# Eight experts of a mixture on one core: three at 128 slots and five at 64 in place of four and four

## The chip, the core and the metric

The kernel runs on one core of a Trainium2 chip. The metric is the device time of one execution in microseconds (us). Before the change the median of three runs is 1869.29 us (1868.2 to 1874.53). The core's engines are TensorE (PE; PEld loads its stationary operand), VectorE (DVE), ScalarE (ACT), GpSimd (POOL) and SyncE (SP), which here only issues loads. A load or store runs on the core's 16 DMA engines.

## The reference

Two layers of a diffusion transformer on 256 latent and 256 context tokens of width 1024, all in 32-bit floating point. The first layer has neighbourhood attention, a convolution and a dense feed-forward block; the second has a state-space mixer and, at its end, a mixture of eight experts on the 256 latent tokens. Only this last part is touched:

```
def moe_swiglu(h, w_router, w1, w3, w2):
    t = h.reshape(-1, shp[-1])                     # 256 x 1024
    logits = t @ w_router                          # 256 x 8
    top_val, top_idx = lax.top_k(logits, 2)
    top_w = jax.nn.softmax(top_val, axis=-1)
    gate = ...                                     # 256 x 8, zero but for two experts per token
    for e in range(8):
        out = out + gate[:, e:e+1] * swiglu(t, w1[e], w3[e], w2[e])

swiglu(h, w1, w3, w2) = (silu(h @ w1) * (h @ w3)) @ w2
```

The weights of an expert are two matrices of 1024 x 3584 and one of 3584 x 1024, 44 MB, so the eight have 352 MB. Each token goes to two experts. With the reference's inputs the experts get 116, 34, 59, 57, 98, 34, 91 and 23 tokens, in the order of the weights.

## The kernel before, in words

**Slots and places.** Each expert's tokens are gathered into a fixed number of slots, 128 or 64. Which place of the program has how many is the table `FEW` (true: 64 slots, here called narrow; false: 128, wide). Place 0 is always expert 0; the other places take the other experts by the number of their tokens. `arrange` ranks the counts on VectorE, `place_rank` holds the rank that each place takes, and `cap` its number of slots. The weights of the places 1 to 7 are loaded by an index that SyncE reads from `cnt` (`moe_src`). What goes beyond the slots of a place is computed in a second pass (`overflow`), which runs only if there is something. Before, `FEW` alternates: places 0, 2, 4 and 6 are wide.

**Steps.** An expert is worked in seven steps, its chunks of 512 hidden columns. A step reads six units of 1 MB: two of w1, two of w3 (the up products) and two of w2 (the down products). The two kinds of step differ:

- In a wide step each unit is split into a rounded high part (ScalarE, line 203) and the rest (mostly VectorE, line 205), and every product is three matmuls with 512 columns (`mm3`, lines 223 to 225): 72 in all. A unit's buffer is free once it is split.
- In a narrow step the units are used as they are, in full 32-bit matmuls. Two of them with 64 stationary columns lie side by side in the array: w1 beside w3 in the up products (line 2022), the two halves of the width in the down products (line 2056). A unit's buffer is free once its matmuls are done.

The list of all steps, `self.steps`, is made in `moe_plan`, and the order of the loads (`seq`) follows from it. In that order a step's w2 units stand after the next step's w1 and w3. Before, the list begins with `LAG` = 2 wide steps and then takes one wide and one narrow step in turn, while there are wide ones. It ends with two narrow steps more.

**Order of the work.** `moe` walks the list. For step i it issues the first up products, the transposes of the hidden values of step i-1 (`turn`), the second up products, and the down products of step i-1 (`finish`). The orders of TensorE, ScalarE, GpSimd and SyncE are those of the program; VectorE's is the scheduler's. `need` splits a wide step's units up to two units ahead. At given chunks of an expert it prepares the next one of its kind: its permutation is turned for the way back at chunk 2 (`way`), the next expert's permutation is built at chunk 4 (`place`, on GpSimd), and its tokens are fetched at chunk 6 (`gather`: lines 1850 wide, 1868 narrow). After an expert's last down products its results are weighted and added back to the residual in six parts (`scatter`, `scatter_few`, matmuls at 1915, 1916 and 1940, additions on VectorE at 1922), one part at each of three calls of `step()` per step.

**Loads.** `Stream` issues every unit from SyncE's queue into the next free buffer (line 85): four of its own and six lent by stages that are done, ten of 1 MB in all in this stage. The queue is strictly in order, and waits where the next buffer isn't free:

```
    def issue(self):
        while self.free and self.at < len(self.specs):
            which = self.free.pop(0)
            ...
                self.nc.sync.dma_start(view, src)
    def release(self, name):
        ...
        self.free.append(which)
        self.issue()
```

Of the kernel before, what the change touches and what calls it, by code (L numbers as in the profile page):

```python
# [9 lines left out]
F32 = mybir.dt.float32  # L10
# [3 lines left out]
OP = mybir.AluOpType  # L14
AX = mybir.AxisListType
P = 128
# [140 lines left out]
class Kernel:  # L157
# [1495 lines left out]
    def route_first(self):  # L1653

        nc, a = self.nc, self.a
        G = nc.gpsimd
        flat = self.pw.rearrange("p a b c -> p (a b c)")
        at = [128]

        def new(*shape):  # L1660
            n = int(np.prod(shape))
            v = flat[:, at[0]:at[0] + n]
            at[0] += n
            return v if len(shape) == 1 else v.rearrange("p (a b) -> p a b", a=shape[0])
        self.iota, self.before, self.ones = new(P), new(P), new(P)
        self.tri, self.router, self.lift = new(8, 8), new(8, 8), new(8, 8)
        self.gate, self.mask, self.pos, self.lg, self.rank = (new(2, 8) for _ in range(5))
        self.base, col, self.ssq, self.v01 = new(8), new(2, 8), new(2, 2), new(2, 2)
        pattern = lambda o, p, m: G.iota(o, pattern=p, base=0, channel_multiplier=m,
                                         allow_small_or_imprecise_dtypes=True)  # L1670
        pattern(self.iota, [[1, P]], 0)
        pattern(self.tri, [[1, 8], [-1, 8]], 0)
        pattern(self.before, [[1, P]], -1)
        G.tensor_scalar(self.tri, self.tri, 0.0, None, op0=OP.is_gt)
        G.tensor_scalar(self.before, self.before, 0.0, None, op0=OP.is_gt)
        G.memset(self.ones, 1.0)
        o = self.s5u.tile([P, 336], F32, name="order")
        self.iota64, self.hot = o[:, 0:P], o[:, P:P + 64].rearrange("p (a b) -> p a b", a=8)
        self.own = [o[:, 192 + 16 * i:208 + 16 * i].rearrange("p (a b) -> p a b", a=2) for i in range(3)]
        self.place_rank, self.cap, self.sums, self.ranks = (o[:, 240 + 8 * i:248 + 8 * i] for i in range(4))  # L1680
        pattern(self.iota64, [[0, 2], [1, 64]], 0)
        pattern(self.place_rank, [[1, 4], [4, 2]], 0)
        G.iota(self.cap, pattern=[[0, 4], [-64, 2]], base=P, channel_multiplier=0, allow_small_or_imprecise_dtypes=True)
        G.tensor_scalar(self.cap[:, 0:1], self.cap[:, 0:1], FIRST, None, op0=OP.add)
        G.dma_start(self.router, a["router"])
        for i in range(2):
            G.dma_start(col[:, i], self.rowsd[i + 1:i + 2].rearrange("a (k p) -> p (a k)", p=P))
        G.tensor_tensor(self.lift, self.router, col[:, 0][:, :, None].to_broadcast([P, 8, 8]), op=OP.mult)
        G.tensor_tensor(self.router, self.router, col[:, 1][:, :, None].to_broadcast([P, 8, 8]), op=OP.mult)
# [146 lines left out]
    def place(self, e, t, beyond=False):  # L1836

        pos, mask = (self.own[i][:, t, e:e + 1] if e or beyond else (self.pos, self.mask)[i][:, t, 0:1] for i in range(2))
        if beyond:
            p = self.wk([P, 1], "ss", 4)  # L1840
            self.nc.gpsimd.tensor_scalar(p, pos, -64.0 if FEW[e] else -float(P), None, op0=OP.add)
            pos = p
        eng = self.nc.gpsimd if e else self.nc.vector
        eng.tensor_scalar(self.perm[:, e % 2, t], self.iota64 if FEW[e] and not beyond else self.iota, pos, mask, op0=OP.is_equal,  # L1844
                          op1=OP.mult)

    def fetch(self, pt, n, t, e=0):

        for i in range(4):
            self.nc.tensor.matmul(pt[:, i * P:(i + 1) * P], lhsT=self.h2[:, t, (4 * n + i) * P:(4 * n + i + 1) * P],  # L1850
                                  rhs=self.perm[:, e % 2, t].bitcast(F32), start=not t and not i, stop=t == 1 and i == 3,
                                  skip_group_check=True)

    def fetched(self, pt, n):
# [18 lines left out]
    def way(self, e):  # L1873

        nc = self.nc
        back = self.back[:, e % 2]
        pt = self.ps("bk")
        for t in range(2):
            nc.tensor.transpose(pt[:, t * P:(t + 1) * P], self.perm[:, e % 2, t].bitcast(F32), self.ident)  # L1879
        nc.scalar.copy(back.rearrange("p a b -> p (a b)"), pt[:, 0:256])  # L1880
        return back

    def gather(self, e, beyond=False):
# [4 lines left out]
        def rest():  # L1888
            if FEW[e] and not beyond:
                self.fetch_few()  # L1890
                return
            for n in range(2):
                pt = self.ps("xT")
                for t in range(2):
                    self.fetch(pt, n, t, e)
                self.fetched(pt, n)
# [70 lines left out]
    def moe_plan(self):  # L1967

        many, few = ([(e, c) for e in range(8) if FEW[e] == i for c in range(7)] for i in range(2))
        self.steps = many[:LAG]  # L1970
        for i, s in enumerate(few):
            self.steps += many[LAG + i:LAG + i + 1] + [s]
        seq, last = [], []
        for e, c in self.steps:
            seq += [(k, e, c, j) for j in range(2) for k in ("m1", "m3")] if FEW[e] else \
                   [(k, e, c, j) for k in ("m1", "m3") for j in range(2)]
            seq += last
            last = [("m2", e, c, j) for j in range(2)]
        seq += last
        for s in seq:  # L1980
            self.st.add(s, partial(self.moe_src, *s))
        self.mseq = seq
        self.expert = {}
# [7 lines left out]
    def moe(self):  # L1991
        nc = self.nc
        seq = self.mseq
        pos = {s: i for i, s in enumerate(seq)}

        def need(name):
            i = pos[name]
            for j in (i, i + 1, i + 2):
                if j < len(seq) and not FEW[seq[j][1]]:
                    self.split(seq[j])  # L2000
# [67 lines left out]
        few = self.hT.rearrange("p k t -> p (k t)")[:, 0:1024].rearrange("p (a b) -> p a b", a=2)  # L2068
        self.few = few[:, 0].rearrange("p (k s) -> p k s", k=8)
        held, y, adds, after = None, {}, [], {}  # L2070
# [6 lines left out]
        def finish(e, c, t):  # L2077
            if not c:
                y[e] = self.ps("y") if FEW[e] else [self.ps("y") for _ in range(2)]
            down(e, c, t, y[e])  # L2080
            if c == 6:
                ready, add = (self.scatter_few if FEW[e] else self.scatter)(e, y.pop(e), self.back[:, e % 2])
                acts = [partial(ready, 0), partial(ready, 1) if FEW[e] else partial(ready, 1, "ntmp")] + \
                       [partial(add, n, (u,)) for n in range(2) for u in range(2)]
                adds.extend([acts[i] for i in v] for v in ADDS)
        end = len(self.steps) - 1
        for i, (e, c) in enumerate(self.steps):
            if FEW[e]:
                o = self.ps("m1")
                up_few(e, c, 0, o)  # L2090
                ready_h = lambda o=o: self.hidden_few(o)
            else:
                p1 = up("m1", e, c)
            step()
            if i:
                t = turn(*held)
            else:
                self.weights()
                self.arrange()
                for p in range(1, 8):  # L2100
                    self.expert[p] = nc.values_load(self.cnt[0:1, 16 + p:17 + p], engines=[mybir.EngineType.SP],
                                                    min_val=0, max_val=7)
            if i == 1:
                after[1] = self.gather(1)
            if c == 2:
                self.way(e)
            if c == 4 and e < 6:
                after[e % 2] = self.gather(e + 2)
            if FEW[e]:
                up_few(e, c, 1, o)  # L2110
            else:
                p3 = up("m3", e, c)
                ready_h = lambda p1=p1, p3=p3: self.hidden(p1, p3)
            step()
            early = not c or i == end
            if early:
                held = e, ready_h()
            if i == LAG:
                after[1]()
            if c == 6 and e < 6:  # L2120
                after[e % 2]()
            if i:
                finish(*self.steps[i - 1], t)
                step()
            if not early:
                held = e, ready_h()
        finish(7, 6, turn(*held))
        while adds:
            step()
# [157 lines left out]
START = ((1, 3), (1, 3), (1, 3), (3, 1))  # L2287
SPLIT1 = (2, 3)

FEW = (False, True) * 4  # L2290

LAG = 2

FIRST = 1024.0

# [27 lines left out]
```

## Time and profile before

| | us |
|---|---|
| median of three runs | 1869.29 |
| profiled execution, its own time | 1870.19 |
| its span, from the first to the last instruction | 1868.4 |
| TensorE busy (8730 matmul records) | 1725.3, 92% |
| VectorE busy | 1249.1, 67% |
| ScalarE busy | 803.0, 43% |
| loads and stores | 517.08 MB, mean 277 GB/s |
| loads of expert weights | 336 units of 1 MB |

Busy shares are means over the whole span. The expert stage is its second half: its first matmul starts at 986.13 us, its first narrow matmul at 1034.7 us. What a change in that stage is worth is read from stretches of it. A matmul record's duration is longer than the distance to the next, as they overlap in the array, so lengths of steps are taken from starts and from the chain of waits. A full 32-bit matmul has two records.

### The profile page before, as it was taken

The page shows a single profiled execution, that of the slowest core. Times are in us where ns is not written, and L with a number is a line of the kernel's source. Part 1 is how long each engine was busy: PE and PEld are TensorE (multiplying, and loading weights), DVE is VectorE, ACT ScalarE, POOL GpSimd, SP SyncE. Part 2 cuts the span into 40 slices and gives each one's busy share as a digit, 9 for nine tenths or more (in the row PEclk, how much of TensorE's full clock was granted, in tenths as well). Part 3 has the DMA queues.
Part 4 walks back from the last instruction along what each step waited for, and adds up shares of the span by engine and source line. Part 5 has one row for each costly group of instructions (what it writes and reads, how often), then busy time and mean ns, then how long its engine had stood idle before and what let it go on. Part 6 is the DMA issues. An engine that isn't in the chain of part 4 may idle for free.

```text
span 1868.4 us, 23796 instructions
## 1 busy us (share of the span) xinstructions
PE 1725.3 (92%) x8730; PEld 1188.6 (64%) x8730; DVE 1249.1 (67%) x1709; ACT 803.0 (43%) x1156; POOL 474.6 (25%) x528
## 2 busy tenths in 40 slices
PE   6977898998989999897589999999999999999997
PEld 4855376876767778675478666556565656565653
DVE  4999797576675754769788565656565656565653
ACT  3434664332332332547456445344543435443540
POOL 2347057395893900245241000000000000000000
PEclk9988999999999999998799999999999999999999
DMA  7320734753645543449868899999999999998996
GB/s 319 131 73 23 278 123 152 255 193 125 220 157 177 194 160 113 160 159 176 251 272 330 340 419 419 404 386 387 420 420 381 385 390 420 417 387 356 407 420 273
DMA packets 107437, 517.08 MB, mean 277 GB/s; under 512 B 13792, under 2 KB 41696, under 8 KB 48688
## 3 DMA queue, kind: packets, MB, share of 16 engines
q1 hardware_dynamic: 76672, 490.77, 68.5%
q10 hardware_dynamic: 29968, 22.57, 3.8%
q0 software_dynamic: 672, 2.14, 0.4%
q8 instruction: 71, 1.16, 0.2%
q14 instruction: 54, 0.44, 0.1%
HBM read 496.46 MB, written 18.97 MB: 276 GB/s over the span
## 4 chain that ended last, share of the span: by engine, by line
PE 56%; DVE 7%; POOL 2%; DMA 2%; issue 1%; ACT 1%; ACTq 0%; SPq 0%; DVEq 0%; POOLq 0%
PE m L2022 11%; PE m L223 5%; PE y L2056 5%; PE m L224 5%; PE m L225 5%; PE y L224 3%; PE y L223 3%; PE y L225 3%; PE w L224 3%; PE w L223 3%; PE w L225 3%; DVE wl L205 1%; PE xT L1850 1%; PE gT L2041 1%; PE sc L1940 1%
## 5 line engine op out<-in xcount | busy, mean ns | idle before, releaser
L203 ACT CAST wh<-raw 128x1024 fp32r<-128x1024 f32 x192 | 194.6, 1049 | 155.1 <-PE w L225 74.7
L205 DVE TENSOR_TENSOR wl<-raw,wh 128x1024 fp32r<-128x1024 f32 x171 | 215.9, 1298 | 37.2 <-ACT wh L203 37.0
L2022 PE MATMUL m<-raw,E 128*64 128x512 f32 x392 | 177.9, 596 | 0.0
L2044 ACT CAST small<-gT 128x512 fp32r<-128x512 f32 x28 | 16.4, 586 | 300.3 <-PE gT L2041 300.3
L224 PE MATMUL w<-hl,wh 128*128 128x512 f32 (+1 forms) x384 | 144.1, 375 | 1.2 <-POOL hl L568 0.6
L223 PE MATMUL w<-hh,wh 128*128 128x512 f32 (+1 forms) x384 | 145.2, 379 | 0.0
L225 PE MATMUL w<-hh,wl 128*128 128x512 f32 (+1 forms) x384 | 142.8, 373 | 0.0
L224 PE MATMUL m<-wl,small 128*128 128x512 f32 x336 | 131.1, 390 | 1.0 <-DVE wl L205 1.0
L223 PE MATMUL m<-wh,small 128*128 128x512 f32 x336 | 131.4, 391 | 0.0
L225 PE MATMUL m<-wh,small 128*128 128x512 f32 x336 | 130.8, 389 | 0.0
L2045 DVE TENSOR_TENSOR small<-gT,small 128x512 fp32r<-128x512 f32 x28 | 19.4, 692 | 156.8 <-ACT small L2044 156.8
L2022 PE MATMUL m<-xres,E 128*64 128x512 f32 x216 | 98.5, 598 | 0.0
L2022 PEld LDWEIGHTS m<-raw,E 128*64 128x64 f32 x392 | 51.0, 137 | 66.5 <-issue 66.4
L1844 POOL TENSOR_SCALAR brow<-pw,order 128x128 fp32r<-128x128 f32 x6 | 5.5, 930 | 310.2 <-PE bk L1879 310.2
L223 PEld LDWEIGHTS w<-hh,wh 128*128 128x128 f32 x384 | 72.7, 189 | 17.3 <-issue 4.0
L224 PEld LDWEIGHTS w<-hl,wh 128*128 128x128 f32 x384 | 72.8, 189 | 15.0 <-POOL hl L568 2.8
L224 PE MATMUL w<-wl,gh 128*128 128x512 f32 x176 | 72.1, 410 | 10.4 <-DVE wl L205 10.4
L225 PEld LDWEIGHTS w<-hh,wl 128*128 128x128 f32 x384 | 72.5, 189 | 12.9
L205 POOL TENSOR_TENSOR wl<-raw,wh 128x1024 fp32r<-128x1024 f32 x21 | 53.2, 2543 | 100.3 <-ACT wh L203 100.3
L205 DVE TENSOR_TENSOR wl<-U,wh 128x1024 fp32r<-128x1024 f32 x55 | 67.3, 1262 | 13.2 <-ACT wh L203 13.1
L223 PE MATMUL w<-wh,gh 128*128 128x512 f32 x176 | 71.8, 408 | 2.0 <-ACT wh L203 2.0
L223 PEld LDWEIGHTS m<-wh,small 128*128 128x128 f32 x336 | 63.1, 188 | 15.2 <-ACT more L203 2.3
(440 smaller groups left out, 4474.1 us busy)
## 6 DMA issues: line engine op xcount, KB each, us to landing
raw<-in_moe SPq DMA_DIRECT2D x134, 1024.0 KB, 10.1
U<-in_moe SPq DMA_DIRECT2D x70, 1024.0 KB, 9.8
room<-in_moe SPq DMA_DIRECT2D x68, 1024.0 KB, 8.4
raw<-in_ada_w SPq DMA_DIRECT2D x48, 1024.0 KB, 5.2
h<-in_moe SPq DMA_DIRECT2D x35, 1024.0 KB, 10.5
raw<-in_ffn_w SPq DMA_DIRECT2D x30, 1024.0 KB, 5.0
xres<-in_moe SPq DMA_DIRECT2D x29, 1024.0 KB, 9.9
raw<-in_mix_w_in SPq DMA_DIRECT2D x10, 1024.0 KB, 6.3
```

What stands on the lines that cost most here:

```text
L203: nc.scalar.copy(wh[:, :m], flat[:, h:h + m])
L205: eng.tensor_tensor(wl[:, :m], flat[:, h:h + m], wh[:, :m].bitcast(F32), op=OP.subtract)
L223: nc.tensor.matmul(o, lhsT=ah, rhs=bh, start=start, stop=False)
L224: nc.tensor.matmul(o, lhsT=ah, rhs=bl, start=False, stop=False)
L225: nc.tensor.matmul(o, lhsT=al, rhs=bh, start=False, stop=stop)
L1850: self.nc.tensor.matmul(pt[:, i * P:(i + 1) * P], lhsT=self.h2[:, t, (4 * n + i) * P:(4 * n + i + 1) * P], rhs=self.perm[:, e % 2, t].bitc ...
L1940: nc.tensor.matmul(po, lhsT=back[r, t].bitcast(F32), rhs=box[0][r], start=True, stop=True)
L2022: nc.tensor.matmul(o[64 * i:64 * i + 64], lhsT=self.few[:, 4 * j + k], rhs=w[i][:, k], start=not j and not k, stop=j == 1 and k == 3, tile ...
L2041: nc.tensor.transpose(pt[:, i * P:(i + 1) * P], g[:, i * P:(i + 1) * P], self.ident)
L2044: nc.scalar.copy(gh, v)
L2045: nc.vector.tensor_tensor(gl, v, gh.bitcast(F32), op=OP.subtract)
L2056: nc.tensor.matmul(y[64 * n:64 * n + 64], lhsT=t[:, 2 * j + f], rhs=w[:, f, n * 512:n * 512 + 512], start=not c and not j and not f, stop= ...
```

## The change

Place 0, 3 and 6 are wide, the places 1, 2, 4, 5 and 7 narrow. The ranks are given out so that the two fullest experts after expert 0 get the wide places. Buffers that were chosen by the place's parity (`perm`, `back`) are chosen by its kind. The steps' list begins with three wide steps; then each next step is of the kind of which the larger share is left. What follows an expert is looked up as the next place of its kind. The turning of the permutation moves to chunk 3, behind a flush of additions that are still pending.

```
         pattern(self.iota64, [[0, 2], [1, 64]], 0)
-        pattern(self.place_rank, [[1, 4], [4, 2]], 0)
-        G.iota(self.cap, pattern=[[0, 4], [-64, 2]], base=P, channel_multiplier=0, ...)
-        G.tensor_scalar(self.cap[:, 0:1], self.cap[:, 0:1], FIRST, None, op0=OP.add)
+        for i, e in enumerate(sorted(range(8), key=lambda e: (FEW[e], e))):
+            G.memset(self.place_rank[:, e:e + 1], float(i))
+        for e in range(8):
+            G.memset(self.cap[:, e:e + 1], 64.0 if FEW[e] else FIRST + P if not e else float(P))
...
-        eng.tensor_scalar(self.perm[:, e % 2, t], ...
+        eng.tensor_scalar(self.perm[:, int(FEW[e]), t], ...
...
-        back = self.back[:, e % 2]
+        back = self.back[:, int(FEW[e])]
...
         self.steps = many[:LAG]
-        for i, s in enumerate(few):
-            self.steps += many[LAG + i:LAG + i + 1] + [s]
+        del many[:LAG]
+        while many or few:
+            self.steps.append((many if len(many) * 7 * sum(FEW) > len(few) * (7 * (8 - sum(FEW)) - LAG) else few).pop(0))
...
+        following = {e: next((f for f in range(e + 1, 8) if FEW[f] == FEW[e]), None) for e in range(8)}
...
-            if c == 2:
+            if c == 3:
+                while adds:
+                    step()
                 self.way(e)
-            if c == 4 and e < 6:
-                after[e % 2] = self.gather(e + 2)
+            if c == 4 and following[e]:
+                after[e] = self.gather(following[e])
...
-            if i == LAG:
-                after[1]()
-            if c == 6 and e < 6:
-                after[e % 2]()
+            if i == LAG - 1:
+                after.pop(1)()
+            if c == 6 and following[e]:
+                after.pop(e)()
...
-FEW = (False, True) * 4
-LAG = 2
+FEW = (False, True, True, False, True, True, False, True)
+LAG = 3
```

Both lists of steps begin in the same way, with three wide steps and a narrow one (W is wide, n narrow, with place and chunk):

```
before  W00 W01 W02 n10 W03 n11 W04 n12 W05 n13 W06 n14 W20 n15 ... W65 n73 W66 n74 n75 n76
after   W00 W01 W02 n10 W03 n11 W04 n12 n13 W05 n14 n15 W06 n16 n20 W30 n21 n22 W31 ... n74 n75 W66 n76
```

ScalarE's order at the place where two narrow steps first follow each other. Its casts at L203 belong to wide steps, `lth` is the activation of a step's hidden values (64 rows in a narrow step), and the copies from `gT` bring transposed hidden values back. Before, from the second narrow step of place 1 on:

```order
L1962 ACTIVATE lth<-m_8831 64x512
L203 CAST more<-U 128x1024 x2
L203 CAST wh<-raw 128x1024 x2
L2038 COPY E_7049<-gT 128x256
L1948 ACTIVATE lth<-m_8923 128x512
L2044 CAST small<-gT 128x512
L1880 CAST brow<-bk 128x256
L203 CAST wh<-U 128x1024 x2
L203 CAST more<-raw 128x1024 x2
L203 CAST wh<-U 128x1024 x2
L203 CAST wh<-raw 128x1024 x2
L1962 ACTIVATE lth<-m_9012 64x512
```

After the change, from the same step on:

```order
L1963 ACTIVATE lth<-m_8844 64x512
L203 CAST more<-U 128x1024 x2
L203 CAST wh<-raw 128x1024 x2
L2040 COPY E_7049<-gT 128x256
L1949 ACTIVATE lth<-m_8936 128x512
L2046 CAST small<-gT 128x512
L203 CAST wh<-U 128x1024 x2
L203 CAST more<-raw 128x1024 x2
L1963 ACTIVATE lth<-m_9025 64x512
L2040 COPY E_7049<-gT 128x256
L1881 CAST brow<-bk 128x256
L203 CAST wh<-U 128x1024 x2
```

A second narrow activation's transposed copy follows the first without the casts of a wide step between them, and the copy of `bk` (the permutation's way back) has moved behind them.

TensorE's order at the end of the stage: `y` are down products, `gT` transposes of hidden values, `sc` at the lines 1915 and 1916 (1916 and 1917 after) the adding back of a wide expert, at 1940 (1941) that of a narrow one. Before, where the lines left out hold one more narrow step's matmuls:

```order
L2036 MATMUL gT<-ident,gt 128x64 x4
...
L1915 MATMUL sc<-ntmp,brow 128x512
L1916 MATMUL sc<-ntmp,brow 128x512
L2056 MATMUL y<-U,E_7049 64x512 x4
L2056 MATMUL y<-raw,E_7049 64x512 x4
...
L1940 MATMUL sc<-adsb,brow 128x512 x4
```

After the change:

```order
L2038 MATMUL gT<-ident,gt 128x64 x4
L2058 MATMUL y<-raw,E_7049 64x512 x4
L2058 MATMUL y<-U,E_7049 64x512 x4
L1916 MATMUL sc<-adsb,brow 128x512
L1917 MATMUL sc<-adsb,brow 128x512
...
L1916 MATMUL sc<-ntmp,brow 128x512
L1917 MATMUL sc<-ntmp,brow 128x512
L1941 MATMUL sc<-adsb,brow 128x512 x4
```

All of place 6's adding back has moved behind the last down products, ahead of place 7's.

## Rows read from the trace of the kernel before

**Rows 1.** The page's part 2: forty slices of the span, busy tenths of the DMA engines.
```profile
DMA  7320734753645543449868899999999999998996
```

**Rows 2.** Stretches: from:to, length, busy us of PE, PEld, DVE, ACT, POOL (instructions), PEclk, DMA share, GB/s.
```profile
1034.70:1852.00 817.30, 802.13 (x3631) 484.81 (x3630) 479.99 (x492) 358.94 (x435) 8.66 (x10) 0.99 0.98 399
1038.00:1852.00 814.00, 798.84 (x3616) 483.80 (x3614) 479.99 (x492) 358.94 (x435) 8.66 (x10) 0.99 0.98 400
```

**Rows 3.** Waits of SyncE's queue from 1110 to 1868 us: total, times, longest.
```profile
SPq L85 <- DVE wl L205: 204.9, 84, 7.3
SPq L85 <- PE y L2056: 159.3, 46, 8.8
```

**Rows 4.** Stretches of 20 us of the expert stage, columns as in rows 2.
```profile
1180.00:1200.00 20.00, 18.07 (x80) 8.62 (x77) 10.17 (x12) 9.04 (x11) 0.00 (x0) 1.00 0.94 381
1200.00:1220.00 20.00, 20.00 (x94) 12.19 (x94) 9.65 (x11) 5.22 (x8) 0.00 (x0) 1.00 1.01 422
...
1460.00:1480.00 20.00, 18.93 (x86) 9.04 (x85) 6.30 (x9) 7.34 (x11) 1.98 (x2) 1.00 1.00 373
...
1820.00:1840.00 20.00, 20.00 (x92) 9.01 (x90) 10.59 (x14) 4.45 (x7) 0.00 (x0) 1.00 1.01 418
1840.00:1860.00 20.00, 18.34 (x82) 6.26 (x78) 6.16 (x9) 1.33 (x3) 0.00 (x0) 1.00 0.49 202
```

**Rows 5.** The chain of waits through one narrow and one wide step: start, us, what.
```profile
1063.22 3.43 PE m L2022 x16
1066.65 0.59 PE gT L2041 x4
1067.24 3.58 PE m L2022 x16
...
1081.93 0.39 PE gT L2036 x4
...
1087.98 3.58 PE y L2056 x16
```

**Rows 6.** The chain at experts' ends (first three rows), then TensorE's timeline at a wide one.
```profile
1144.91 3.57 PE xT L1850 x32
...
1223.03 3.72 PE xT L1868 x32
...
1255.13 1.07 PE sc L1940 x2
...
1412.43 0.51 PE L1915 MATMUL sc<-ntmp,brow 128*128 128x512 f32 x1
...
1413.01 0.39 PE L223 MATMUL y<-wh,small 128*128 128x512 f32 x1
```

**Rows 7.** SyncE's timeline: the first issue after the start of the narrow steps.
```profile
1038.33 0.34 SPq L85 DMA_DIRECT2D U<-in_moe  x1
```

**Rows 8.** The end of the chain of waits: start, us, what.
```profile
1852.38 3.68 PE y L2056 x16
...
1858.86 2.05 DVE xres L1922 x3
```

**Rows 9.** ScalarE's timeline and the chain: the copies and subtractions of one unit.
```profile
1227.26 2.00 ACT L203 CAST wh<-U 128x1024 fp32r<-128x1024 f32 x2
...
1256.88 2.36 DVE wl L205 x2
```

**Rows 10.** GpSimd: a fill of 128x8, and the instruction that follows the routing tables.
```profile
L325 POOL MEMSET mhalf<- 128x8 f32 x1 | 0.1, 104 | 0.0
...
863.67 1.32 POOL L1345 TENSOR_TENSOR brow<-L,power 128x512 f32<-128x512 f32 x1 [39.07 <-ACT L L1300]
```

**Rows 11.** TensorE's timeline behind a short wait: start, us of a record, what, [idle before].
```profile
1415.15 0.50 PE L224 MATMUL y<-wl,small 128*128 128x512 f32 x1 [1.75 <-DVE wl L205]
...
1416.88 0.63 PE L225 MATMUL y<-wh,small 128*128 128x512 f32 x1
...
1419.74 0.39 PE L223 MATMUL y<-more,small 128*128 128x512 f32 x1
```

More of the change, by code (lines that the diff above doesn't have):

```diff
@@ L1681, in route_first @@
         pattern(self.iota64, [[0, 2], [1, 64]], 0)
-        pattern(self.place_rank, [[1, 4], [4, 2]], 0)
-        G.iota(self.cap, pattern=[[0, 4], [-64, 2]], base=P, channel_multiplier=0, allow_small_or_imprecise_dtypes=True)
-        G.tensor_scalar(self.cap[:, 0:1], self.cap[:, 0:1], FIRST, None, op0=OP.add)
+        for i, e in enumerate(sorted(range(8), key=lambda e: (FEW[e], e))):
+            G.memset(self.place_rank[:, e:e + 1], float(i))
+        for e in range(8):
+            G.memset(self.cap[:, e:e + 1], 64.0 if FEW[e] else FIRST + P if not e else float(P))
         G.dma_start(self.router, a["router"])
@@ L1843, in place @@
         eng = self.nc.gpsimd if e else self.nc.vector
-        eng.tensor_scalar(self.perm[:, e % 2, t], self.iota64 if FEW[e] and not beyond else self.iota, pos, mask, op0=OP.is_equal,
+        eng.tensor_scalar(self.perm[:, int(FEW[e]), t], self.iota64 if FEW[e] and not beyond else self.iota, pos, mask, op0=OP.is_equal,
                           op1=OP.mult)
@@ L1850, in fetch @@
             self.nc.tensor.matmul(pt[:, i * P:(i + 1) * P], lhsT=self.h2[:, t, (4 * n + i) * P:(4 * n + i + 1) * P],
-                                  rhs=self.perm[:, e % 2, t].bitcast(F32), start=not t and not i, stop=t == 1 and i == 3,
+                                  rhs=self.perm[:, int(FEW[e]), t].bitcast(F32), start=not t and not i, stop=t == 1 and i == 3,
                                   skip_group_check=True)
@@ L1875, in way @@
         nc = self.nc
-        back = self.back[:, e % 2]
+        back = self.back[:, int(FEW[e])]
         pt = self.ps("bk")
         for t in range(2):
-            nc.tensor.transpose(pt[:, t * P:(t + 1) * P], self.perm[:, e % 2, t].bitcast(F32), self.ident)
+            nc.tensor.transpose(pt[:, t * P:(t + 1) * P], self.perm[:, int(FEW[e]), t].bitcast(F32), self.ident)
         nc.scalar.copy(back.rearrange("p a b -> p (a b)"), pt[:, 0:256])
@@ L2081, in finish @@
             if c == 6:
-                ready, add = (self.scatter_few if FEW[e] else self.scatter)(e, y.pop(e), self.back[:, e % 2])
+                ready, add = (self.scatter_few if FEW[e] else self.scatter)(e, y.pop(e), self.back[:, int(FEW[e])])
                 acts = [partial(ready, 0), partial(ready, 1) if FEW[e] else partial(ready, 1, "ntmp")] + \
```

## The prediction, made before the changed kernel was run

> **What bounds the kernel now.** I read the page's slices first. The line of the DMA engines shows the place: from the twenty-third slice on, which is the expert stage, it stands at 8 or 9 tenths until the last slice [rows 1]. The stretches of that stage say more. From the first narrow matmul at 1034.7 us to 1852 us TensorE is busy for 802.13 of 817.30 us at a granted clock of 0.99 (2.4 GHz but for moments), while the DMA engines are busy for 0.98 of the time and move 399 to 400 GB/s [rows 2]. So two engines are nearly full, and the question is which of them has room when the other gets less to do. TensorE is the one that sets the end: in the waits of this stretch no compute engine is released last by a load, and SyncE's own queue waits for buffers to come free, 204.9 us behind VectorE's splits and 159.3 us behind TensorE's matmuls of the narrow experts [rows 3]. Loads wait for compute, not the other way round.
>
> How much room have the loads? Of the forty stretches of 20 us from 1040 to 1840 us, thirty show a DMA share of 0.99 or more. Twenty-four of those thirty run at 418 to 422 GB/s, the lowest at 373; their mean is 415.5. The other ten, such as the one after 1180 us (share 0.94, 381 GB/s), are those in which the queue waited for a buffer [rows 4]. A rate of 418 lies between that mean and the usual 420, and I take it for a queue that never waits; 415.5 and 422 are kept as ends. So the loads have some 4.5% in hand (400 against 418), no more.
>
> **What the change does to TensorE.** It swaps one expert of 128 slots for one of 64: seven wide steps go, seven narrow ones come. The chain of waits gives both lengths, because it runs through TensorE alone in mid-expert. A narrow step is its first half of the up products, 3.43 us, its second half, 3.58, its down products, 3.58, and the four transposes of its hidden values, 0.39: 10.98 us. A wide step is what lies between the end of the narrow one's second half (1067.24 + 3.58 = 1070.82) and 1087.98, that is 17.16 us, less the narrow transposes (0.39) that fall into it, with its own (0.59) added: 17.36 us [rows 5]. The difference is 6.38 us, seven times 44.7 us. An expert's ends differ too: fetching its tokens takes 3.57 us wide and 3.72 narrow. Adding it back takes four narrow matmuls at some 1.07 us (4.3 us) where the wide has four pairs; a pair took 0.58 us (1412.43 to 1413.01), 2.3 us in all [rows 6]. That gives back 2.1 us. TensorE's path shrinks by 42.6 us, if its 15 us of waits stay.
>
> **What it does to the loads: nothing in bytes.** A 64-slot expert still reads all its weights, and a step reads six units of 1 MB (1.049 million bytes) either way. At 418 GB/s six units take 15.05 us: less than a wide step (17.36), more than a narrow one (10.98). One narrow and one wide, as before, take 28.3 us on TensorE and 30.1 on the queue. The new run of two narrow and one wide takes 39.3 us and 45.2. TensorE's work at the experts' ends, 5.9 to 8.0 us each, gives the queue time to catch up, some 50 us at the seven still to come, and the ten buffers hold another 25 us of loads. That covered 1.8 us a pair. It can't cover 5.9 us in each of sixteen such runs, 94 us. So the loads end last after the change, and I sum along them.
>
> The start is the same in both, three wide steps, and at 1038.33 us the queue issues again after standing still for the narrow buffers, with everything ahead loaded [rows 7]. From 1038 to 1852 us it moves 400 GB/s x 814 us = 325.6 MB [rows 2]. At 418 that is 779 us; from 1039 us on, the last unit lands at 1818 us. In the kernel before it landed at 1840 + 20 x 202/420 = 1849.6 us [rows 4]. By the ends of the rate it is 1810.6 (422) or 1822.6 (415.5).
>
> Does the queue stand still again? A stretch like that after 1180 us loses 20 x (420 - 381)/420 = 1.9 us. None is the lower bound; one at each of the six changes of expert still to come, 11 us, the upper. I take one, 2 us, because each run of three steps draws the stock down by 5.9 us.
>
> **The end.** Before, the last down products end at 1852.38 + 3.68 = 1856.06 us, 6.5 us after the last landing, and 12.3 us before the end at 1868.4 [rows 8]. After, the last units are those of the last narrow step, and the two before them belong to the last wide one. The second of those lands two units (5.0 us) earlier, its copy takes 2.00 us and its subtraction 2.36 [rows 9], its twelve matmuls 2.8 (a wide step's 72 take 17.36 - 0.59 us, 0.23 each), then 0.8 for the transposes and copy, then 3.7: 6.7 us after the last landing, the same as before. But expert 6's adding back, which before lay among the last narrow steps, now stands between the last down products and the last expert's own. VectorE does those four additions in order: a first pair of matmuls of 0.6 us, then four additions at 2.05/3 = 0.7 each [rows 8], 3.4 us more. The ends are 0, if they get in ahead of the down products, and 5.
>
> **Small parts.** Sixteen one-column fills replace two patterns and an addition on GpSimd at 816 us. A 128x8 fill took 104 ns, so 1.7 us come and some 0.5 go; GpSimd has nothing due until 863.67 us, 39.07 us of idle time [rows 10]. If that cover went, it would cost 1 us. The back transposes that move from chunk 2 to chunk 3 and the tables indexed by kind keep their work and their engine: no cost, at most a 0.4 us transpose later. The flush ahead of them waits for additions that, at three steps of the list per chunk, have all gone by chunk 3 in this order, so nothing queues behind it.
>
> **The sum.** 1818 + 2 + 6.7 + 12.3 + 3.4 = 1842.4 us of span. The profiled execution took 1870.19 with a span of 1868.4, and the median of the three runs is 1869.29, 0.9 above that span. So 1843 us, 26 us or 1.4% less. A difference of 0.3% (5.6 us) is about what a measurement of this kernel can tell from no change.
>
> The loads' rate carries the sum, so a rule against it counts. The rows show 418 to 422 GB/s with the queue full [rows 4]. The Trainium skill, *DMA: Bandwidth & Descriptors*, section "Where 436 GB/s comes from", holds that loads from HBM are bound by the memory side at about 358 GB/s for a core. By it the loads could have no room, and the trace disagrees: this core already moves 400 on average [rows 2].
>
> **Rivals.**
> *TensorE stays the bound.* The loads run at 422, or the stock lasts longer. Then the path is 1868.4 - 42.6 + 3.4 = 1829.2, so 1830 us. For it: the work at experts' ends gives the queue time. Against: 45.2 us of loads to 39.3 of matmuls. Chance 0.12.
> *The wide steps start late (slower).* When the stock is gone, a wide step's first unit comes just in time, and TensorE waits for copy and subtraction, 4.36 us [rows 9]. Behind such a wait the array is slow: after 1.75 us of idling that end at 1415.15, matmul records last 0.63 us instead of 0.39 from 1416.88 until short of 1419.74, so of 2.9 us at 1.2 GHz instead of 2.4 half is lost, 1.4 us [rows 11]. With the 4.36 that is 5.8 us at each of eighteen wide starts, 104 us, 1934 us in all. Up to 0.7 us a start hides behind the loads (13 us between 1830 and 1843); from 2.2 us a start the whole gain is gone, from 2.5 it is slower by over 0.3%. Against: narrow steps before it need neither split, so ScalarE and VectorE can run ahead, and a late TensorE lets the stock refill. Chance of a small part of it (1848 to 1863) 0.15, of no change 0.06, of slower 0.04. The Trainium skill, *TensorE: Matmul & The Clock Gate*, section "HAM oscillation — how this bites in real kernels", says that waiting for loads between bursts throws the array back to half rate again and again; the rows agree that one short wait does it, and by that alone the sum would rise by 18 x 1.4 = 25 us on TensorE, 13 of them hidden.
> *It doesn't fit.* A fourth expert with over 64 tokens would be computed again after the stage, its 42 units loaded anew: 105 us at the least, over 1940 us. The inputs of the reference send 116 tokens to expert 0, then 98, 91, 59, 57, 34, 34 and 23; 59 fits. Chance 0.02.
> *The memory gives less than the queue asks.* If long saturation brought the rate down to 358, the loads would take 909 us and the end come at 1972. Only rows of 20 us could speak for it, none of them a saturated one below 373. Chance 0.01. (This is the page's rule above.)
>
> **How the numbers follow.** My forecast, 1833 to 1857 by its ends, has 0.60. The range from 1829 to 1859 takes in the first rival and about half of the small late starts: 0.60 + 0.12 + 0.08. Faster by over 0.3%: 0.60 + 0.12 + 0.15 = 0.87; within 0.3%: 0.06; slower: 0.04 + 0.02 + 0.01 = 0.07.
>
> **What would show it.** Right: 20 us stretches from some 1150 us on at 415 to 420 GB/s with a share of 1.0 throughout, TensorE's busy time in the stage down by about 40 us while its idle time grows from 15 to 25 or more, idle time before narrow matmuls or splits that loads end, a last landing near 1818 us, and some 3 us more between the last down products and the end. Wrong: DMA shares of 0.9 with TensorE full (the first rival), or a granted clock below 0.95 with DMA shares under 1 (the second), or the rows of a second pass.

## The result, and the profile after the change

The changed kernel takes 1848.66 us (median of four runs, 1846.59 to 1849.86) beside 1871.56 us for the kernel before (median of four, 1868.2 to 1874.53). The ratio is 0.9874, with a 95% interval of 0.986 to 0.9888: 22.9 us less, where the prediction had 26. A second set of runs gave 1846.1 beside 1873.03 us, ratio 0.9862 (0.9847 to 0.9877). The predicted 1843 us is 3 to 6 us too low, and the range of 1829 to 1859 holds both medians. The loads have the same bytes, 517.03 MB for 517.08.

The first lines to look at are the page's: the DMA engines in forty slices of the span, and under it the GB/s of the same slices:

```profile
DMA  8320743664653653357966899999999999999995
GB/s 320 126 83 23 245 154 139 211 217 145 226 177 119 215 185 114 144 179 142 290 275 232 327 421 420 419 420 420 419 420 420 420 419 398 404 419 421 419 420 225
```

Of the kernel before, [rows 1] has the first line; its GB/s are

```profile
GB/s 319 131 73 23 278 123 152 255 193 125 220 157 177 194 160 113 160 159 176 251 272 330 340 419 419 404 386 387 420 420 381 385 390 420 417 387 356 407 420 273
```

In the line of tenths only one slice shows the change, the thirty-seventh, at 8 before and 9 after. The GB/s show it plainly: from the twenty-fourth slice to the last but one they lay anywhere between 356 and 420, and are 419 to 421 now but for two slices, 398 and 404. The stretches say the same in numbers. The kernel before, from 1045 to 1800 us (length, busy time of PE, PEld, DVE, ACT and POOL with their records, PE's granted clock, DMA share, GB/s):

```profile
1045.00:1800.00 755.00, 739.91 (x3349) 456.04 (x3348) 452.38 (x462) 342.16 (x412) 8.66 (x10) 0.99 0.98 401
```

The changed kernel, the same stretch and some of 20 and 5 us:

```profile
1045.00:1800.00 755.00, 731.84 (x3310) 400.26 (x3309) 356.15 (x374) 263.57 (x333) 12.86 (x12) 0.99 1.01 417
1180.00:1200.00 20.00, 20.00 (x108) 11.40 (x104) 9.14 (x11) 6.68 (x9) 0.00 (x0) 1.00 1.01 419
1540.00:1560.00 20.00, 18.45 (x79) 8.24 (x77) 6.90 (x9) 4.86 (x6) 0.00 (x0) 0.98 0.97 392
1560.00:1580.00 20.00, 20.00 (x79) 8.91 (x78) 8.39 (x10) 6.53 (x8) 0.00 (x0) 0.94 0.94 376
1780.00:1800.00 20.00, 17.78 (x80) 10.25 (x79) 6.14 (x8) 6.56 (x8) 0.00 (x0) 1.00 1.01 422
...
1820.00:1825.00 5.00, 4.07 (x17) 2.91 (x17) 4.78 (x5) 3.06 (x4) 0.00 (x0) 1.00 0.70 290
```

The stretch after 1180 us, in which the queue waited for a buffer before [rows 4], now runs at 419 GB/s. TensorE's idle time grew from 15 us (755 - 739.91) to 23, less than the prediction's 25. The last landing is read from the last row: 290 of 419 GB/s fill 3.5 of its 5 us, so 1823.5 us, an estimate, where the kernel before had 1849.6 by the same reckoning.

Who waits for whom has turned round. Before, a load was the last to release a compute engine three times in the stage, 0.3 us each (TensorE's weight loads); the prediction's "no compute engine" is right but for these 0.9 us. After (engine, line, what it waited for: us in total, times, longest; from 1038 to 1848 us):

```profile
ACT wh L203 <- DMA raw<-in_moe: 24.1, 12, 6.6
ACT wh L203 <- DMA xres<-in_moe: 12.6, 7, 7.2
ACT wh L203 <- DMA U<-in_moe: 11.2, 4, 7.2
ACT wh L203 <- DMA room<-in_moe: 10.7, 7, 2.9
```

ScalarE, which makes the first copy of a wide step's unit, waits 59 us for units that have not landed. The end of the chain of waits goes through such a unit (start, us, what; `wh` and `wl` are the split of a unit, `y` down products, `gT` transposes of hidden values, `sc` and `xres` the adding back):

```profile
1799.27 19.29 DMA room<-in_moe
1818.56 0.02 issue
1818.58 1.05 ACT wh L203
...
1819.66 2.37 DVE wl L205 x2
...
1825.60 0.70 DVE gt L1908
...
1826.32 0.70 DVE gt L1965
...
1827.16 0.45 PE gT L2038 x4
...
1828.05 3.65 PE y L2058 x16
1831.70 0.43 PE sc L1916
...
1832.40 2.73 DVE xres L1923 x4
1835.12 0.60 DVE adsb L1935
...
1835.77 2.04 PE sc L1941 x6
```

The unit `room` is the last one of the wide step W66. It lands at 1818.56 us, 5 us ahead of the last landing. Its split, W66's down products and the last narrow step's take until 1831.70. Then place 6 is added back (L1916, L1923) ahead of place 7 (L1935, L1941), as the order of the changed kernel says, and the span ends 15.8 us after the last down products (before: 12.3, [rows 8]).

For all runs one table helps. The stage's queue stands still for a while and then issues again: at 1038.33 us before [rows 7]. That issue is the zero point, since everything that the change touches lies behind it. Times in us; landing (estimated as above; not read for `half_before`), down products and end are counted from that issue, in the profiled execution.

| kernel | median | queue issues again at | last landing | last down products end | span ends |
|---|---|---|---|---|---|
| before | 1871.56; 1873.03 | 1038.33 | 811.3 | 817.7 | 830.1 |
| as predicted | 1843 | 1038.33 | 781.7 | 788.4 | 804.1 |
| after | 1848.66 | 1041.14 | 782.4 | 790.6 | 806.4 |
| `after_again` | 1846.1 | 1037.51 | 779.3 | 789.6 | 806.5 |
| `half_before` | 1871.09 | 1038.94 | - | 818.6 | 831.1 |
| `half_after` | 1819.41 | 1035.13 | 748.7 | 765.1 | 780.8 |
| `two_wide` | 1840.14 | 1040.83 | 777.7 | 785.6 | 798.1 |
| `alternate` | 1857.99 | 1045.21 | 798.4 | 803.9 | 816.5 |
| `tail` | 1842.45 | 1039.32 | 781.9 | 787.1 | 800.8 |
| `so_vec` | 1842.93 | 1034.92 | 782.3 | 790.9 | 806.7 |
| `both` | 1835.22 | 1033.58 | 779.9 | 785.8 | 799.8 |

### The profile page after: what moved, and what is told of

It is laid out like the page before. It is cut to its first block, busy times and chain, and to the rows that moved or that the text cites. A ratio compares the mean times of both kernels' runs of the same rounds, so it can differ in the third digit from the quotient of the medians.

```text
span 1847.5 us, 23203 instructions
## 1 busy us (share of the span) xinstructions
PE 1690.4 (91%) x8562; PEld 1122.3 (61%) x8562; DVE 1144.5 (62%) x1614; ACT 719.8 (39%) x1069; POOL 475.3 (26%) x541
## 2 busy tenths in 40 slices
DMA packets 107432, 517.03 MB, mean 280 GB/s; under 512 B 13792, under 2 KB 41696, under 8 KB 48688
## 4 chain that ended last, share of the span: by engine, by line
PE 43%; DMA 12%; DVE 7%; POOL 2%; ACT 1%; issue 1%; SPq 0%; ACTq 0%; DVEq 0%; POOLq 0%
PE m L2024 10%; PE y L2058 5%; DMA U<-in_moe 4%; PE m L223 3%; PE m L224 3%; PE m L225 3%; DMA room<-in_moe 3%; PE w L223 2%; PE w L225 2%; PE w L224 2%; DMA raw<-in_moe 2%; PE y L224 2%; PE y L223 2%; PE y L225 2%; DVE wl L205 1%
## 5 line engine op out<-in xcount | busy, mean ns | idle before, releaser
L205 DVE TENSOR_TENSOR wl<-raw,wh 128x1024 fp32r<-128x1024 f32 x151 | 192.4, 1309 | 93.2 <-ACT wh L203 93.2
L203 ACT CAST wh<-raw 128x1024 fp32r<-128x1024 f32 x172 | 173.6, 1048 | 172.2 <-PE w L225 73.9
L1845 POOL TENSOR_SCALAR brow<-order 128x128 fp32r<-128x128 f32 x10 | 9.3, 941 | 473.9 <-PE bk L1880 462.4
L224 PE MATMUL m<-wl,small 128*128 128x512 f32 x252 | 100.9, 401 | 9.7 <-DVE wl L205 9.7
L223 PE MATMUL m<-wh,small 128*128 128x512 f32 x252 | 101.6, 403 | 4.8 <-ACT wh L203 4.8
L2024 PE MATMUL m<-U,E 128*64 128x512 f32 x232 | 105.4, 597 | 0.0
L225 PE MATMUL m<-wh,small 128*128 128x512 f32 x252 | 100.0, 397 | 0.0
L2046 ACT CAST small<-gT 128x512 fp32r<-128x512 f32 x21 | 12.3, 586 | 221.8 <-PE gT L2043 221.8
L2047 DVE TENSOR_TENSOR small<-gT,small 128x512 fp32r<-128x512 f32 x21 | 14.5, 692 | 131.8 <-ACT small L2046 131.8
L2024 PE MATMUL m<-room,E 128*64 128x512 f32 x208 | 94.4, 597 | 0.0
L2040 ACT COPY E<-gT 128x256 f32<-128x256 f32 x35 | 13.0, 371 | 160.1 <-PE gT L2038 160.1
## 6 DMA issues: line engine op xcount, KB each, us to landing
room<-in_moe SPq DMA_DIRECT2D x66, 1024.0 KB, 13.1
```

Of the source, the lines that this page charges most:

```text
L203: nc.scalar.copy(wh[:, :m], flat[:, h:h + m])
L205: eng.tensor_tensor(wl[:, :m], flat[:, h:h + m], wh[:, :m].bitcast(F32), op=OP.subtract)
L223: nc.tensor.matmul(o, lhsT=ah, rhs=bh, start=start, stop=False)
L224: nc.tensor.matmul(o, lhsT=ah, rhs=bl, start=False, stop=False)
L225: nc.tensor.matmul(o, lhsT=al, rhs=bh, start=False, stop=stop)
L1845: eng.tensor_scalar(self.perm[:, int(FEW[e]), t], self.iota64 if FEW[e] and not beyond else self.iota, pos, mask, op0=OP.is_equal, op1=OP. ...
```

## The experiments

**Fewer bytes, the same matmuls (`half_after`, `half_before`).** The first question is which engine sets the end. The edit cuts the loads of a narrow step's w2 units by half and leaves every instruction of the engines in place:

```
-                self.nc.sync.dma_start(view, src)
+                if name[0] == "m2" and FEW[name[1]]:
+                    self.nc.sync.dma_start(view[:, :, 0:512], src[:, :, 0:512])
+                else:
+                    self.nc.sync.dma_start(view, src)
...
-                            nc.tensor.matmul(y[64 * n:64 * n + 64], lhsT=t[:, 2 * j + f], rhs=w[:, f, n * 512:n * 512 + 512],
+                            nc.tensor.matmul(y[64 * n:64 * n + 64], lhsT=t[:, 2 * j + f], rhs=w[:, f, 0:512],
```

> The changed kernel with half of each w2 unit of the narrow places left unloaded (70 units of 0.5 MB; the second half of the width is multiplied with the first half's weights, so the narrow experts' results are not the reference's). TensorE's work is the same, the loads have 36.7 MB less, 87 us at 420 GB/s. Loads set the end (my theory): the bound passes to TensorE, 1833 us, from 1828 to 1838. Rival, TensorE and its waits set the end already: 1849, no change beyond 3 us.

The same cut in the kernel before:

> The same cut in the kernel before (56 units of 0.5 MB, 29.4 MB or 70 us of loads less; the same part of the results left out). My theory, there TensorE sets the end: 1870, no more than 5 us faster. Rival, the loads were the bound of the kernel before as well: 1840 or less.

Measured: `half_after` 1819.41 us (1817.78 to 1825.97), ratio to the kernel before 0.9738 (0.9716 to 0.9759), 29 us less than the changed kernel. `half_before` 1871.09, ratio 0.9996 (0.9986 to 1.0005): the same bytes taken away from the kernel before are worth nothing. Of the 29 us, 25.6 lie behind the queue's restart (780.8 for 806.4); the rest lies ahead of it, where the two programs do the same work and executions differ. So the bound was TensorE and is now the loads. In `half_after` TensorE is the bound again, and the loads have room (380 GB/s):

```profile
1045.00:1800.00 755.00, 744.74 (x3416) 401.43 (x3414) 366.82 (x386) 264.82 (x340) 12.89 (x12) 1.00 0.95 380
```

Its time is 14 us below what I expected, outside the range. TensorE's own path after the change is much shorter than I had put it; the next section says by how much.

**Fewer matmuls, the same bytes (`two_wide`).** Place 6 becomes narrow too, and no second pass runs:

```
-            G.memset(self.cap[:, e:e + 1], 64.0 if FEW[e] else FIRST + P if not e else float(P))
+            G.memset(self.cap[:, e:e + 1], 1024.0 if FEW[e] else FIRST + P if not e else float(P))
...
-FEW = (False, True, True, False, True, True, False, True)
+FEW = (False, True, True, False, True, True, True, True)
```

> The changed kernel with two wide places (0 and 3) and six narrow ones, the limit of a narrow place raised so that no second pass runs: 27 of the 91 tokens of the third fullest expert are left out. TensorE has another 42 us less, the loads the same bytes. Loads set the end: 1849, from 1844 to 1854. TensorE sets it: 1806.

Measured: 1840.14 us (1838.66 to 1842.37), ratio 0.9837 (0.982 to 0.9853). That is 4 us below the range expected if loads set the end, and 34 above the rival. Another seven wide steps gone are worth 8.5 us, not the 43 that TensorE's path would give. The table says where the 8.5 come from: the DMA engines never run short between 1045 and 1800 us (419 GB/s for 417), so that the last unit lands 4.7 us earlier after the queue's restart (777.7 for 782.4); the last down products follow 7.9 us behind it (8.2); and the end 12.5 us behind these, not 15.8, as no wide place's results wait to be added there. Against the changed kernel's repetition (`after_again` below) the landing gives less, 1.6 us, and the work behind it more. The stretch:

```profile
1045.00:1800.00 755.00, 722.53 (x3176) 352.36 (x3178) 265.41 (x292) 188.65 (x254) 10.76 (x12) 0.98 1.01 419
```

TensorE is idle for 32 us of it, and the loads lose nothing by that.

**The order alone (`alternate`).** The same three and five experts, but after the first three wide steps one narrow and one wide in turn, as in the kernel before, and seventeen narrow steps alone at the end.

```
-        while many or few:
-            self.steps.append((many if len(many) * 7 * sum(FEW) > len(few) * (7 * (8 - sum(FEW)) - LAG) else few).pop(0))
+        for i, s in enumerate(few):
+            self.steps += [s] + many[i:i + 1]
```

> The changed kernel with one narrow and one wide step in turn after the first three, as before the change, so that 17 narrow steps stand alone at the end. The same work and the same bytes. My theory: in the alternating part TensorE is the bound and the queue stands still now and then (568 us for 18 pairs, as before), then 92 units at 2.5 us follow for the narrow steps: 1865, from 1857 to 1873. Rival, the order of the steps doesn't matter as long as all is in: 1849.

Measured: 1857.99 us (1853.21 to 1863.44), ratio 0.9924 (0.9906 to 0.9942), 9 us above the changed kernel and inside the expected range, at its lower end. Two of its stretches:

```profile
1280.00:1300.00 20.00, 20.00 (x92) 10.20 (x91) 9.41 (x11) 6.44 (x9) 3.24 (x2) 1.00 0.93 354
...
1820.00:1840.00 20.00, 17.14 (x72) 5.68 (x72) 1.37 (x2) 1.33 (x3) 0.00 (x0) 1.00 1.01 418
```

While wide and narrow steps alternate, TensorE is full and the queue waits (354 GB/s); when only narrow steps are left, the queue is full and TensorE waits. The last unit lands 16 us later after the restart than in the changed kernel (798.4 for 782.4). So merging in proportion is worth 16 us of loading time here; 10 of them reach the end, since with narrow steps alone at the end the down products end 2.7 us sooner behind the last unit (5.5 for 8.2) and the program 3.2 us sooner behind these (12.6 for 15.8). A further 4 us of its profiled time is a later start (1045.21 us), of which more below.

**The end of the list (`tail`).** The last wide step is moved one place forward: `... n74 W66 n75 n76`.

```
+        i = self.steps.index((6, 6))
+        self.steps[i - 1:i + 1] = self.steps[i], self.steps[i - 1]
```

> The same units and the same TensorE work, only the last wide step stands third from the end and not second. My theory of the end: the last load lands at the same time (1823.6 in the trace), but what follows is shorter, since place 6's results are added back behind the last narrow steps and no longer behind the last down products: these end 6.5 us after the last landing and not 8.1, and the program ends 12.4 us after them and not 15.8. So 5 us less, 1844 (1842 to 1846). Rival, in which the loads alone set the end and the work behind them runs beside it, or the wide step's later buffers hold the last loads: no change, 1848 to 1850.

It ran beside a repetition of the changed kernel:

> The changed kernel once more, beside the three below on the same chip: 1848.7 us (1846.6 to 1849.9), 22 to 24 us under the kernel before.

Measured: `tail` 1842.45 us (1839.83 to 1843.52), ratio 0.9837 (0.9824 to 0.9851); `after_again` 1846.1 (1845.87 to 1848.15). Medians 3.7 us apart, and from the queue's restart to the end 5.7 us less (800.8 for 806.5). The last unit lands at the same point (781.9; 779.3 to 782.4 in the others with these units). The down products end 5.2 us after it, 6.5 expected, and the program 13.7 us after them, 12.4 expected. At the end of `tail` TensorE runs from W66's down products to the last ones with no wait but 0.5 us for a copy:

```profile
1800.51 1.05 ACT wh L203
...
1808.83 3.58 PE m L2026 x16
...
1817.67 3.58 PE y L2060 x16
...
1822.76 3.68 PE y L2060 x16
```

So the place at the end of the chain that I named is the right one.

**The start (`so_vec`).** The profiled execution of the changed kernel starts its expert stage 3 us late: TensorE's first matmul in it at 989.15 us for 986.13, the queue's restart at 1041.14 for 1038.33. Some 75 us earlier VectorE computes a table of powers, products of 128x512 of 0.69 us. Two of them are four times as long in the changed kernel (VectorE's timeline: start, us):

```profile
911.36 0.69 DVE L1345 TENSOR_TENSOR ntmp<-T,power 128x512 f32<-128x512 f32 x1
...
914.01 0.69 DVE L1345 TENSOR_TENSOR ntmp<-T,power 128x512 f32<-128x512 f32 x1
914.62 2.89 DVE L1346 TENSOR_TENSOR ntmp<-T,power 128x512 f32<-128x512 f32 x1
917.44 2.88 DVE L1347 TENSOR_TENSOR ntmp<-ntmp,L 128x512 f32<-128x512 f32 x1
920.36 0.69 DVE L1348 TENSOR_TENSOR T<-ntmp 128x512 f32<-128x512 f32 x1
```

Beside them GpSimd subtracts the two halves of a weight unit (the changed kernel, GpSimd's timeline):

```profile
914.43 5.34 POOL L205 TENSOR_TENSOR wl<-raw,wh 128x1024 fp32r<-128x1024 f32 x2 [23.21 <-ACT wh L203]
```

ScalarE's copies of the result (L1328, L1329) and then TensorE wait for the L1348 at the end of this. The experiment gives the two subtractions to VectorE, by taking the name `('so', 1, 0, 0)` out of both sets of `ON_POOL`; in VectorE's order they stand behind the products.

> The two subtractions of one earlier weight unit (at 914 us, 2.7 us each) go from GpSimd to VectorE, behind the power-table products. My theory: the two products that took 2.9 us beside them take 0.69, the result that ScalarE's copies wait for is there 4.4 us earlier (916.7 for 921.1), the stage of the experts starts up to 4 us earlier (first matmul of it 985 to 987, 989.2 in the trace of the changed kernel; first load behind the stand-still 1037 to 1039, 1041.1) and the whole is as much shorter: 1845 (1844 to 1847). Rival 1: the long products have another cause (their operands, or ScalarE beside them) and stay at 2.9 us: 1848 to 1851, since VectorE has 2.4 us more. Rival 2: they shrink, but another wait holds the stage's start: 1848 to 1849.

Measured: 1842.93 us (1839.61 to 1844.2), ratio 0.9837 (0.9823 to 0.9851), 3.2 us under `after_again` and 1 us below the expected range. All the products take 0.69 us now (VectorE's timeline of `so_vec`):

```profile
912.06 0.69 DVE L1345 TENSOR_TENSOR ntmp<-T,power 128x512 f32<-128x512 f32 x1
...
914.72 0.69 DVE L1345 TENSOR_TENSOR ntmp<-T,power 128x512 f32<-128x512 f32 x1
915.32 0.68 DVE L1346 TENSOR_TENSOR ntmp<-T,power 128x512 f32<-128x512 f32 x1
...
919.91 2.35 DVE L205 TENSOR_TENSOR wl<-raw,wh 128x1024 fp32r<-128x1024 f32 x2
```

TensorE's wait, in the changed kernel's trace

```profile
928.98 3.64 PE L1475 MATMUL y<-raw,T 128*32 128x128 f32 x64 [6.26 <-ACT T L1329]
```

becomes, in `so_vec`,

```profile
925.54 1.96 PE L1475 MATMUL y<-raw,T 128*32 128x128 f32 x64 [1.57 <-ACT T L1329]
```

The queue restarts at 1034.92 us, and what lies behind is as long as in the changed kernel (806.7 for 806.4). The restart by itself is weak evidence, since executions differ: it fell between 1035.13 and 1045.21 us in the traces that keep this work on GpSimd. Every one of these has two long products, `half_after` too, which restarted at 1035.13 us, so most of that spread comes from elsewhere. It lies largely ahead of the table, whose first product of 128x512 starts anywhere between 906.3 and 916.6 us. Counted from that product to TensorE's L1475 above, the traces agree: 13.5 us in `so_vec` (925.54 - 912.06) and in `both`, 17.3 to 17.6 in the six changed kernels with the pair on GpSimd (928.98 - 911.36 in the first), 16.0 in `before` and `half_before`. So the pair on GpSimd costs some 4 us here. Which two products are hit depends on an execution's timing: in `after_again` GpSimd's pair began at 910.88 us, and the products that took 2.77 us were an L1348 and an L1345, as in the kernel before. The cost was there before the change too; whether the 1.3 to 1.6 us by which all six lie above the kernel before belong to the change is open.

**Both edits (`both`).**

> The two edits above in one kernel. My theory: they act at different places on a path that the loads set, so their gains add: 1840 (1837 to 1843). Rival, where either is hidden by the loads: 1844 to 1848.

Measured: 1835.22 us (1833.63 to 1839.17), ratio to the kernel before 0.9804 (0.9789 to 0.9819): 10.9 us under `after_again`, 2 us below the expected range and the best of all with the full work. The two gains by themselves are 3.7 and 3.2 us; the rest, 4 us, is no larger than the ranges of these runs, so that I read no third effect into it. From restart to end it has 799.8 us, `tail`'s 800.8.

## Why the prediction was right

**What bounds it.** Right, and shown from both sides: a cut of bytes alone moves the changed kernel by 26 to 29 us and the kernel before by nothing, and a cut of matmuls alone moves the changed kernel by 8.5.

**The loads' term, 779 + 2 us.** Right. From the queue's restart to the last landing I had 781.7 us; the changed kernel's two executions show 782.4 and 779.3. The rate was a little better than the 418 taken (418 to 422 in nearly every stretch of 20 us), and the loads ran short at a few places. The one taken at 2 us was there, at the change of expert about 1530 us. There VectorE first works on the results of the place that ends, and its subtraction for the wide step comes behind that (TensorE's timeline of the changed kernel: start, us, what, [idle before]):

```profile
1529.16 0.79 PE L224 MATMUL m<-wl,small 128*128 128x512 f32 x1 [2.94 <-DVE wl L205]
1529.75 0.63 PE L225 MATMUL m<-wh,small 128*128 128x512 f32 x1
```

Records of 0.63 us as in [rows 11] follow until about 1535 us: TensorE at a granted clock of 0.50, 1.2 GHz, behind a wait of 2.94 us. The three stretches of 20 us from 1540 to 1600 us then run at 392, 376 and 406 GB/s and lose some 4 us. In `after_again` the same wait is there, but the records behind it keep to 0.39 us:

```profile
1525.73 0.50 PE L224 MATMUL m<-wl,small 128*128 128x512 f32 x1 [2.94 <-DVE wl L205]
1526.07 0.40 PE L225 MATMUL m<-wh,small 128*128 128x512 f32 x1
```

There the three stretches ran at 408, 412 and 419, and lost 1. That the slow records are what cost the other 3 us fits these two executions, but isn't tested. This is the second rival, in a small part. Its price per start, with 1.4 us for the clock each time, was too general: the clock fell behind some waits and not behind others of the same length. In the changed kernel it stayed at 1.00 behind another wait of 2.94 us, at 1212.34, and in the kernel before it stayed at 1.00 behind a wait of 1.75 us at 1194.38 and fell behind the one at 1415.15. And most waits cost the loads nothing: in the 20 us around the wait at 1212.34 they ran at 421 GB/s. The first rival's place, TensorE, was far from deciding; its price was wrong (below). The fourth rival fell: the queue kept 417 GB/s for 755 us. The Trainium skill, *DMA: Bandwidth & Descriptors*, section "Where 436 GB/s comes from", has the memory side bind at about 358 GB/s; this trace does not bear that out, and long saturation did not bring it about.

**TensorE's path, -42.6 us.** This was the term furthest off, though it did not decide. The sum for TensorE alone was 42.6 less the 3.4 of the end, 39.2 us; `half_after`, in which TensorE is the bound, took 49.3 us off the stretch behind the restart (830.1 to 780.8). The stretches from the restart to the end, of the kernel before and of `half_after`, say what it is made of:

```profile
1038.33:1868.40 830.07, 804.93 (x3638) 485.98 (x3638) 484.18 (x498) 359.27 (x435) 8.66 (x10) 0.99 0.97 394
1035.13:1815.90 780.77, 759.56 (x3476) 409.71 (x3472) 381.10 (x403) 273.24 (x349) 12.89 (x12) 0.99 0.93 372
```

TensorE's busy time fell by 45.4 us, so steps and experts' ends are worth 2.8 us more than I had summed. Its idle time fell by 3.9, although the end behind the last down products grew by 3.3 (15.7 for 12.4): the waits ahead of it, which I let stay, lost some 7 us. The first rival's 1830 us should have been about 1820.

**The last landing to the last down products, 6.7 us.** Too small: 8.2 in the changed kernel, and 10.3 in its repetition, where the wide unit landed only 2.9 us ahead of the last one. The step that was mis-sized is the sequence behind that unit. I had 2.00 + 2.36 + 2.8 + 0.8 + 3.7 = 11.7 us from its landing. The chain shows 13.1: the subtraction starts when half the copy is done (0.9 less), the down products take 3.5 us rather than 2.8 (0.7 more), and two products on VectorE, 0.70 us each (L1908 for place 6's results, L1965 for the hidden values), stand between the down products and the transposes (1.6 more, with their gaps). I had left these out.

**The end, 12.3 + 3.4 = 15.7 us.** Right: 15.8 us, 16.9 in the repetition. The four additions ahead of place 7's take 2.73 us in the chain, 3.4 with what leads to them, as summed. `tail` shows that 2.1 of these can be had back by moving one step.

**The start, "the same in both".** Right for the program, not for one execution: 1041.14 and 1037.51 us for the 1038.33 that I summed from. Of the 5.1 us between the predicted span (1842.4) and the measured one (1847.5), 2.8 are this, and 2.3 lie behind the restart, 1.5 of them between the last landing and the last down products. In the repetition there was some luck in the sum: the down products ended 3.6 us later behind the last landing than summed, but that landing came 2.4 us sooner.

## What to carry to other kernels

When two engines are both over 95% busy in a stage, an edit that relieves one is worth at most the distance to the other: here 49 us off TensorE's path bought 23. Which of them sets the end, and by how much, is seen by cutting one engine's work alone (here half the bytes of some units), before and after. And a program that is bound by its loads can still gain at its start and its end: here the order of the last steps and one unit's subtractions moved to another engine brought 11 us together, with the same bytes.

## What the runs showed of the hardware

VectorE's product of two operands in SBUF took 0.69 us alone and 2.77 to 2.92 us beside GpSimd's subtraction, ending about half a microsecond behind one of its two halves (some 2.7 us each), and 0.69 again when GpSimd's work was gone. The Trainium skill, *SBUF — State Buffer*, section "SBUF: two separate sides", says that a VectorE instruction with two SBUF inputs and a GpSimd instruction that reads SBUF exclude each other for the whole of an instruction. The trace agrees: the products don't share, they wait.

Long saturation cost the loads nothing: one queue with ten buffers of 1 MB gave 419 GB/s over 755 us (`two_wide`), as fast as the full stretches of 20 us before the change. With several loads in flight a single unit took up to 20 us from issue to landing (`room`, 19.29 us in the chain above). How far ahead of the last one a given unit lands varies between executions: W66's last unit, 5.0 us in one and 2.9 in the other.
